# Gates and branch products of a hybrid trunk computed with tokens on the partitions, on one Trainium2 core

## The chip, the cores and the metric

The kernel runs on one core of one Trainium2 chip, as one program. The metric is the device time of one execution in microseconds (us). Three runs of the kernel before took 1461.19 to 1462.02 us, median 1461.55 us.

## The reference

A trunk of two layers over 256 tokens of width 1024, all in float32. Each layer is a half-weighted SwiGLU block, a mixer of three branches, and a second SwiGLU block. The mixer, cut to what matters:

```python
h = rms_norm(x, mix_norm[l])
rg_x, rg_g, sb_q, sb_k, sb_v, c_q, c_kv, k_r, gate_logits = split(h @ w_in[l])
y_a = rg_lru(conv(rg_x), ...) * gelu(rg_g)              # 1024 wide, a linear recurrence over tokens
y_b = stick_breaking_attention(sb_q, sb_k, sb_v)        # 8 heads of 128
y_c = mla_branch(c_q, c_kv, k_r, ...)                   # 8 heads, latent q and kv
g_a, g_b, g_c = split(sigmoid(gate_logits), 3)          # 1024 wide each
merged = g_a * (y_a @ w_branch_a) + g_b * (y_b @ w_branch_b) + g_c * (y_c @ w_branch_c)
x = x + merged @ w_out[l]
```

## The kernel before

Every float32 product is made of three products of split operands: a value is cast to a shorter one (`hi`) and the rest is kept (`lo`), and hi·hi, hi·lo and lo·hi are added. Weights come by DMA as one stream of tiles `raw`, four blocks of 128x512 at a time. For each pair of blocks (a piece) ScalarE casts `hi` and VectorE subtracts `lo` (`split_to`, `next_sub`), two pieces ahead of use. A block is called a sub.

TensorE's work is a list of groups. A feature group (`feature_group`) makes 256 output features with the features on the partitions: for each 128 of the contraction two matmuls of 512 columns (the weight's hi against the activations' hi and lo side by side) and two of 256 columns (the weight's lo against the activations' hi), so 32 matmuls for a contraction of 1024. Its two halves of the result are added at evacuation: a ScalarE copy, a VectorE add. A token group (`token_group`) makes 512 features with the tokens on the partitions: for each 128 of the contraction and each half of the tokens three matmuls of 512 columns (`mm3`), so 48 for a contraction of 1024, and the sum is complete in PSUM. Groups use two accumulators `acc` in turn; a group with a contraction of 256, and the last group of a stage, use two of four small banks `side`.

In the mixer, `MIX_ORDER` is a written-out order of the groups: `v`, `k`, `q`, `rgx`, `rgg`, `cq`, `ckv` from h; `uq`, `uqr`, `ukv`, `uv` from the latents; gates `ga`, `gb`, `gc`; branch products `bra`, `brb`, `brc`; `out`. The last digit is the number of the group. The three branches' own chains (`rg_chain`, `stick_pair`, `mla_pair`) run beside the groups as side tasks: their small matmuls, transposes, activations and vector work are issued between the groups' matmuls. What is issued when is decided while the program is built, by a clock of estimated costs (`Clock`, `Op`): after each step of a group `Tasks.tick` lets a side task issue an operation if its inputs are estimated to be ready, and at most a small amount of TensorE side work. Two calls issue side work without that test: `Tasks.wait`, when a group needs two `side` banks and fewer are free (`small_banks`), and `Tasks.drain`, when a group needs an operand that a task has not yet issued. On the chip each engine runs its instructions in the issued order and waits at each for its operands.

In `mix`, `gate(b, n)` evacuates a gate group, scales it by the norm's factor spread over partitions (`rb`) and takes tanh; `branch(i, b, n)` evacuates a branch product, forms (tanh + 1) times it and adds it to `merged[n]`; at the last branch of a group (i == 2) it casts and subtracts the sum into `mT[n]`, the operand pair of `out`. `update_x` adds an `out` group to x. Nearly all instructions carry the line of one helper, L201.

Of the kernel before, what the change touches and what calls it, by code (L numbers as in the profile page):

```python
# [6 lines left out]
F32 = mybir.dt.float32  # L7
# [7 lines left out]
NT = S // 128  # L15
# [13 lines left out]


MIX_ORDER = tuple((x.rstrip("0123"), int(x[-1])) for x in """
v0 k0 rgx0 rgx1 k1 q0 q1 cq0 q2 q3 k2 rgx2 v1 k3 rgx3 rgg0 rgg1 rgg2 rgg3
gb0 uq0 gb1 uq1 gb2 uq2 gb3 uq3 uqr0 brb0 brb1 ckv0 brb2 brb3 ga0 ukv0 ga1 ukv1 uv0 ga2 ukv2
ga3 ukv3 bra0 bra1 uv1 gc0 bra2 gc1 gc2 gc3 brc0 brc1 brc2 brc3 bra3 out0 out1 out2 out3
""".split())
C_C, C_G = 5120, 5696

FEATURES = {
    "rgx": ("in", 0, KD), "rgg": ("in", 1024, KD), "q": ("in", 2048, KD), "k": ("in", 3072, KD), "cq": ("in", C_C, KD),
    "ga": ("in", C_G, KD), "gb": ("in", C_G + 1024, KD), "gc": ("in", C_G + 2048, KD),  # L40
    "uq": ("uq", 0, 2), "ukv": ("ukv", 0, 2), "bra": ("bra", 0, KD), "brb": ("brb", 0, KD), "brc": ("brc", 0, KD), "out": ("out", 0, KD),
    "dn1": ("dn1", 0, KF), "dn2": ("dn2", 0, KF),
}
TOKENS = {"last": ("dn2", 0, KF), "v": ("in", 4096, KD), "uqr": ("uq", 1024, 2), "uv": ("ukv", 1024, 2)}


def group_stream(what, n):

    if what == "ckv":
        for k in range(0, 9, 3):  # L50
            yield ("ckv0", "in", k, C_C + 256)
            yield ("ckv1", "in", k, C_C + 256)
    elif what in TOKENS:
        m, c, nk = TOKENS[what]
        for k in range(nk):
            yield ("one", m, k, c + 512 * n)
    elif what in FEATURES:
        m, c, nk = FEATURES[what]
        for k in range(0, nk, 2):
            yield ("two", m, k, c + 256 * n)  # L60
    else:
        for k in range(0, KD, 2):
            yield ("gu", what, k, 128 * n)
# [274 lines left out]
def trunk(tc, xT_in, pos_in, w_in, rgw_in, fin_in, const_in, out):  # L338
# [4 lines left out]
    with ctx:  # L343
# [110 lines left out]
        def two(ap):  # L454
            return ap.rearrange("p (j t) -> p j t", j=2)
# [55 lines left out]
        def feature_group(kts, evac, last=0):  # L511


            nk = len(kts)
            a = small_banks() if last or nk <= 2 else bank()
            held = []
            for i, (h, _, hl) in enumerate(kts):
                if i % 2 == 0:
                    wh, wl = next_sub()
                held.append((i, h, hl, wh, wl))  # L520
                if nk - last <= i < nk - 1:
                    continue
# [8 lines left out]
            return finish(evac, a, tasks.LAST if last else None)  # L531

        def plain_group(c, xg, evac, norm):

# [656 lines left out]
        def mix(nm, ntasks, nxt, l):  # L1191
# [49 lines left out]
            merged, sig, mT = {}, {}, {}  # L1241

            def gate(b, n):
                def sigmoid(f):

                    act.activation(out=f, in_=f, func=AF.Tanh, scale=0.5)
                    yield
                    sig[b, n] = f

                def run(a):  # L1250
                    f = yield from scaled(a, mx["nm"], "rb")
                    yield
                    tasks.spawn(sigmoid(f))
                return run

            def branch(i, b, n):

                def run(a):
                    f = yield from FT.take()
                    hl = (yield from RT.take()) if i == 2 else None  # L1260
                    while (b, n) not in sig or (i and n not in merged):
                        yield 1
                    s = sig.pop((b, n))
                    m = merged[n] if i else None
                    for c, ap in parts(a):
                        fc, sc = two(f)[:, c], two(s)[:, c]
                        act.copy(fc, ap[:, :, 256:512])
                        dve.tensor_tensor(fc, ap[:, :, 0:256], fc, op=ALU.add)
                        if type(a) is not list:
                            yield  # L1270
                            give_banks(a)
                        dve.scalar_tensor_tensor(out=fc, in0=sc, scalar=1.0, in1=fc, op0=ALU.add, op1=ALU.mult)
                        if i:
                            mc = two(m)[:, c]
                            dve.tensor_tensor(mc, mc, fc, op=ALU.add)
                        if i == 2:
                            act.copy(hl[:, c, 0], mc)
                            dve.tensor_tensor(hl[:, c, 1], mc, hl[:, c, 0].bitcast(F32), op=ALU.subtract)
                    yield
                    if type(a) is list:  # L1280
                        give_banks(a)
                    FT.give(s)
                    if i == 0:
                        merged[n] = f
                        return
                    FT.give(f)
                    if i == 2:
                        FT.give(m)
                        mT[n] = hl
                return run  # L1290

            branches = [x for x in MIX_ORDER if x[0] in ("bra", "brb", "brc")]
# [14 lines left out]
            for g in MIX_ORDER:  # L1307
                what, n = g
                if what == "cq":
                    lt.append(narrow_group(kts, 256, w_cq, latents(mx, 0)))  # L1310
                elif what == "ckv":
                    lt.append(narrow_group(kts, 320, w_ckv, latents(mx, 1)))
                elif what == "uq":
                    feature_group(Latent(0), head_T(mx, "qn", n, "rbq"))
                elif what == "uqr":
                    token_group(Latent(0), q_rope(mx))
                elif what == "ukv":
                    feature_group(Latent(1), head_T(mx, "kn", n, "rbkv"))
                elif what == "uv":
                    token_group(Latent(1), head_v(mx, "v_ml", n, mx["rkv"]))  # L1320
                elif what == "rgx":
                    feature_group(kts, rg_x(mx, n))
                elif what == "rgg":
                    feature_group(kts, rg_g(mx, n))
                elif what == "v":
                    token_group(kts, head_v(mx, "v_sb", n, mx["rcol"]))
                elif what in ("q", "k"):
                    feature_group(kts, head_T(mx, what, n, "rb", SB_SCALE if what == "q" else None))
                elif what in ys:
                    mtask[n] = feature_group(Pairs(mx[ys[what]], lambda p: work[what][p:p + 1] if what == "bra" else work[what], KD), branch(turn[g], what[2], n), last=4 if g == branches[-1] else 0)  # L1330
                elif what == "out":
                    out_tasks.append(feature_group(Pairs(mT, lambda p: [mtask[p]], KD), lambda a, n=n: update_x(n, a, 0.5, nxt), last=4 if n == 3 else 0))
                else:
                    feature_group(kts, gate(what[1], n))
                if what in ys and n == 3:
# [182 lines left out]
```

## Time and profile before

| what | value |
|---|---|
| median of three runs | 1461.55 us |
| profiled execution, its own time | 1463.23 us |
| its span (first to last instruction) | 1461.4 us |
| TensorE matmul busy | 1442.5 us, 8276 matmuls |
| VectorE busy | 1108.8 us, 1548 instructions |
| ScalarE busy | 888.8 us, 1365 instructions |
| granted TensorE clock | 0.998 of full |
| mixer of layer 1, of layer 2 (from the first `v` matmul to the end of `out3`) | 349.92 us, 350.09 us |

A matmul's end is modelled in this profile and matmuls overlap, so a matmul's cost is read from the distance between starts and not from its busy time. Idle time of an engine is given with what ended it. The two mixers run the same program; the rows below are of the first one where it isn't said otherwise.

### The profile page before, as it was taken

The numbers are of one execution on the slowest core, as the hardware profiler recorded it, in microseconds if no ns is written. First come the engines' busy times: TensorE is split into PE (matmuls) and PEld (weight loads), VectorE is DVE, ScalarE is ACT, GpSimd is POOL, SyncE is SP. The second block draws the span as 40 slices with busy tenths as digits, with TensorE's granted clock in tenths as the row PEclk, the third lists the DMA queues.
The fourth block names the chain that finished last, engine by engine and source line by source line (L and its number), as shares of the span: only waits on it lengthen the run. The fifth ranks groups of instructions, "written<-read, shape, count | busy, mean of one in ns | idle before, by whom it ended". The sixth has DMA issues, their size and how long they took to land.

```text
span 1461.4 us, 20833 instructions
## 1 busy us (share of the span) xinstructions
PE 1442.5 (99%) x8276; PEld 1261.0 (86%) x8276; DVE 1108.8 (76%) x1548; ACT 888.8 (61%) x1365; POOL 144.5 (10%) x118
## 2 busy tenths in 40 slices
PE   8999999999999999999999999999999999999998
PEld 7888889888888888888888888898888888888886
DVE  5887567689987788876677776676989877877853
ACT  4665446888665556555455554479885656566543
POOL 2000001123410000000000000111323000100001
PEclk9999999999999999999999999999999999999999
DMA  6555554444543455455545455544444434545452
GB/s 244 201 185 192 200 179 163 170 151 147 197 148 145 171 179 194 179 200 178 198 173 201 177 198 184 200 159 155 141 171 174 173 138 166 199 175 201 176 199 87
DMA packets 37506, 258.17 MB, mean 177 GB/s; under 512 B 4256, under 2 KB 4640, under 8 KB 6816
## 3 DMA queue, kind: packets, MB, share of 16 engines
q1 hardware_dynamic: 35856, 253.16, 48.0%
q0 software_dynamic: 832, 2.62, 0.6%
q8 instruction: 65, 1.06, 0.3%
q10 hardware_dynamic: 720, 1.05, 0.2%
q14 instruction: 33, 0.27, 0.1%
HBM read 255.77 MB, written 1.05 MB: 176 GB/s over the span
## 4 chain that ended last, share of the span: by engine, by line
PE 90%; DVE 7%; issue 1%; ACT 1%; DMA 0%; ACTq 0%; POOLq 0%; POOL 0%; DVEq 0%
PE acc L201 76%; PE side L201 14%; DVE f L201 3%; DVE lo L201 3%; DVE r L201 1%; DMA x<-xT 0%; ACT f L201 0%; ACT hi L201 0%; ACT r L201 0%; ACTq L396 0%; POOLq L1514 0%; POOL rms L201 0%; DVE rms L201 0%; DVEq L201 0%
## 5 line engine op out<-in xcount | busy, mean ns | idle before, releaser
L201 PE MATMUL acc<-r,hi 128*128 128x512 f32 x3116 | 1000.3, 402 | 0.0
L201 DVE TENSOR_TENSOR lo<-raw,hi 128x1024 fp32r<-128x1024 f32 (+1 forms) x478 | 591.4, 1239 | 231.4 <-ACT hi L201 230.2
L201 PEld LDWEIGHTS acc<-r,lo 128*128 128x128 f32 x3116 | 585.2, 188 | 137.7
L201 PE MATMUL acc<-r,lo 128*128 128x256 f32 x3116 | 613.4, 278 | 0.0
L201 ACT CAST hi<-raw 128x1024 fp32r<-128x1024 f32 (+1 forms) x478 | 496.9, 1045 | 128.8 <-PE acc L201 91.9
L201 PEld LDWEIGHTS acc<-r,hi 128*128 128x128 f32 x3116 | 481.5, 189 | 5.0
L201 POOL TENSOR_TENSOR f<-f,f 128x512 f32<-128x512 f32 (+1 forms) x51 | 90.9, 1787 | 1043.3 <-ACT f L201 959.9
L201 ACT COPY f<-acc 128x512 f32<-128x512 f32 x164 | 96.0, 585 | 121.4 <-PE acc L201 121.2
L201 ACT ACTIVATE f<-f 128x256 f32<-128x256 f32 (+3 forms) x190 | 94.9, 502 | 85.6 <-DVE f L201 84.4
L201 DVE TENSOR_TENSOR f<-acc,f 128x512 f32<-128x512 f32 x166 | 113.9, 686 | 41.6 <-ACT f L201 41.2
L201 DVE TENSOR_TENSOR f<-f,f 128x512 f32<-128x512 f32 (+1 forms) x177 | 125.0, 706 | 7.8 <-ACT f L201 1.6
L201 ACT CAST r<-f 128x256 fp32r<-128x256 f32 (+2 forms) x130 | 58.7, 456 | 63.4 <-DVE f L201 59.7
L201 PE MATMUL acc<-hi,r 128*128 128x512 f32 (+2 forms) x344 | 96.9, 358 | 0.0
L201 PE MATMUL side<-r,hi 128*128 128x512 f32 x260 | 84.5, 396 | 0.0
L201 PE MATMUL side<-f,f 128*128 128x256 f32 (+1 forms) x320 | 71.7, 328 | 0.0
L201 PEld LDWEIGHTS acc<-hi,r 128*128 128x128 f32 x344 | 61.6, 189 | 8.3
L201 DVE TENSOR_TENSOR r<-f,r 128x256 fp32r<-128x256 f32 (+2 forms) x130 | 64.7, 502 | 1.9 <-ACT r L201 1.9
L201 PE MATMUL acc<-lo,r 128*128 128x512 f32 (+2 forms) x172 | 61.0, 355 | 0.0
L201 PE MATMUL side<-r,lo 128*128 128x256 f32 x260 | 60.5, 279 | 0.0
L201 PEld LDWEIGHTS side<-r,hi 128*128 128x128 f32 x260 | 45.6, 188 | 7.5
L201 PEld LDWEIGHTS side<-r,lo 128*128 128x128 f32 x260 | 47.0, 188 | 4.0
L201 PEld LDWEIGHTS side<-f,f 128*128 128x128 f32 x320 | 46.0, 191 | 0.5
(95 smaller groups left out, 839.1 us busy)
## 6 DMA issues: line engine op xcount, KB each, us to landing
raw<-w SPq DMA_DIRECT2D x239, 1024.0 KB, 4.8
f<-rgw POOLq DMA_DIRECT2D x8, 256.0 KB, 3.6
raw<-w SPq DMA_DIRECT2D x4, 256.0 KB, 5.7
out<-f SPq DMA_DIRECT2D x4, 256.0 KB, 2.2
x<-xT ACTq DMA_DIRECT2D x3, 256.0 KB, 6.9
f<-fin POOLq DMA_DIRECT2D x2, 256.0 KB, 3.4
cst<-const SPq DMA_DIRECT2D x1, 336.0 KB, 8.3
x<-xT ACTq DMA_DIRECT2D x2, 128.0 KB, 3.8
```

Of the source, the lines that this page charges most:

```text
L201: return self.f(*self.args, **self.kw)
```

## The change

Gates and branch products become token groups, two of 512 features each instead of four of 256. `gate` evacuates each half of the tokens with one ScalarE copy scaled by a per-token column and takes tanh. `branch` forms (tanh + 1) times the product straight from PSUM, and adds. At the last branch the sum, which has tokens on the partitions, is transposed by TensorE (`transpose_pair`, four 128x128 transposes into a `side` bank for each 256 features), and then cast and subtracted. `out0` and `out1` become one step, `outs0` (`feature_pair`): the first half of the contraction for both, then the second half for both. The order of the groups is new.

```diff
 MIX_ORDER = ...
-... rgg0 rgg1 rgg2 rgg3 / gb0 uq0 gb1 uq1 gb2 uq2 gb3 uq3 uqr0 brb0 ...
+... rgg0 rgg1 uq0 rgg2 uq1 rgg3 uq2 / gb0 uq3 gb1 uqr0 brb0 ckv0 brb1 ...
+        def feature_pair(kts, evacs):
+            nk = len(kts)
+            a = [bank() for _ in range(2)]
+            it = iter(kts)
+            for f in range(2):
+                half = [next(it) for _ in range(nk // 2)]
+                for n in range(2):
+                    for i, (h, _, hl) in enumerate(half, f * nk // 2):
...
+                        for b, c in enumerate(cs_):
+                            pe.matmul(a[n][:, b], wh[:, c], hl, start=i == 0, stop=False, skip_group_check=True)
+                        for b, c in enumerate(cs_):
+                            pe.matmul(a[n][:, b, 0:256], wl[:, c], h, start=False, stop=i == nk - 1, skip_group_check=True)
+                        tasks.tick()
+            return [finish(e, x) for e, x in zip(evacs, a)]
             def gate(b, n):
...
                 def run(a):
-                    f = yield from scaled(a, mx["nm"], "rb")
-                    yield
-                    tasks.spawn(sigmoid(f))
+                    fs = []
+                    for t in range(NT):
+                        f = yield from FT.take()
+                        act.activation(out=f, in_=bank_of(a, t), func=AF.Copy, scale=mx["rcol"][t])
+                        fs.append(f)
+                    yield
+                    give_banks(a)
+                    tasks.spawn(sigmoid(fs))
             def branch(i, b, n):
...
-                    for c, ap in parts(a):
-                        fc, sc = two(f)[:, c], two(s)[:, c]
-                        act.copy(fc, ap[:, :, 256:512])
-                        dve.tensor_tensor(fc, ap[:, :, 0:256], fc, op=ALU.add)
...
-                        if i == 2:
-                            act.copy(hl[:, c, 0], mc)
-                            dve.tensor_tensor(hl[:, c, 1], mc, hl[:, c, 0].bitcast(F32), op=ALU.subtract)
+                    for t, f in enumerate(fs):
+                        dve.scalar_tensor_tensor(out=f, in0=f, scalar=1.0, in1=bank_of(a, t), op0=ALU.add, op1=ALU.mult)
+                        if i:
+                            dve.tensor_tensor(merged[n][t], merged[n][t], f, op=ALU.add)
...
+                    if i == 2:
+                        for q in range(2):
+                            x = yield from transpose_pair(merged[n], q * 256)
+                            hl = yield from RT.take()
+                            hilo(x, hl)
+                            yield
+                            side.give(x)
+                            mT[2 * n + q] = hl
```

The first place is TensorE's order after the group `rgg1` of the first layer. `acc` is a group's accumulator, `side1_87` and `side3_89` are small banks in which two heads of the stick-breaking branch are summed, `r10_100` is a head's split operand that VectorE makes, `f6_112` and `f35_141` are what ScalarE makes of the two banks by an exponential, and `f12`, `f13` are values. Before:

```order
L201 MATMUL acc1_85<-r2_92,hi_2780 128x512 x2
L201 MATMUL acc1_85<-r2_92,lo_2781 128x256 x2
L201 MATMUL acc0_84<-r15_105,hi_2813 128x512 x2
L201 MATMUL acc0_84<-r15_105,lo_2814 128x256 x2
L201 MATMUL acc0_84<-r15_105,hi_2813 128x512 x2
L201 MATMUL acc0_84<-r15_105,lo_2814 128x256 x2
L201 MATMUL acc0_84<-r0_90,hi_2813 128x512 x2
L201 MATMUL acc0_84<-r0_90,lo_2814 128x256 x2
L201 MATMUL acc0_84<-r0_90,hi_2813 128x512 x2
L201 MATMUL acc0_84<-r0_90,lo_2814 128x256 x2
```

Here the whole group `rgg2` (32 matmuls into `acc0`) follows, and the two heads' matmuls stand singly at its end and within `rgg3`. The same place after, where L208 is the same helper:

```order
L208 MATMUL acc1_85<-r2_92,hi_2780 128x512 x2
L208 MATMUL acc1_85<-r2_92,lo_2781 128x256 x2
L208 MATMUL side1_87<-r6_96,tri_r_75 128x384 x2
L208 MATMUL side1_87<-f22_128,cst_72 128x128
L208 MATMUL side3_89<-r10_100,tri_r_75 128x384 x2
L208 MATMUL side3_89<-f27_133,cst_72 128x128
L208 MATMUL side2_88<-f35_141,f12_118 128x256
L208 MATMUL side2_88<-f35_141,f13_119 128x128
L208 MATMUL side2_88<-f6_112,f12_118 128x256
L208 MATMUL side2_88<-f6_112,f13_119 128x128
L208 MATMUL side1_87<-r11_101,hi_2813 128x512
L208 MATMUL side3_89<-r11_101,hi_2813 128x512
```

The ten side operations of two heads now stand in one piece ahead of `uq0`, whose matmuls are the last two rows and take the two banks that the heads give up; nothing of a large group lies between.

The second place is TensorE's order where the merged sums go into `out`. Before, the operands of `out0` (`r15`, `r0`) were made one to four groups earlier, and the last branch group `bra3` ends right ahead of it:

```order
L201 MATMUL side3_89<-r4_94,lo_4794 128x256 x2
L201 MATMUL side3_89<-r10_100,lo_4794 128x256 x2
L201 MATMUL acc1_85<-r15_105,hi_4817 128x512 x2
L201 MATMUL acc1_85<-r15_105,lo_4818 128x256 x2
L201 MATMUL acc1_85<-r15_105,hi_4817 128x512 x2
L201 MATMUL acc1_85<-r15_105,lo_4818 128x256 x2
```

After, the stretch is inside `outs0`, 28 matmuls behind its start; `f23_129` and `f12_118` are the merged sums of the second 512 features for the two halves of the tokens, `r4_94` is the first split operand made of them, and `cst` holds the identity:

```order
L208 MATMUL acc1_85<-r14_104,lo_4398 128x256 x2
L208 MATMUL side1_87<-cst_72,f23_129 128x128
L208 MATMUL acc1_85<-r14_104,hi_4397 128x512 x2
L208 MATMUL acc1_85<-r14_104,lo_4398 128x256 x2
L208 MATMUL side1_87<-cst_72,f12_118 128x128
L208 MATMUL side1_87<-cst_72,f23_129 128x128
L208 MATMUL side1_87<-cst_72,f12_118 128x128
L208 MATMUL side0_86<-cst_72,f23_129 128x128
L208 MATMUL side0_86<-cst_72,f12_118 128x128
L208 MATMUL side0_86<-cst_72,f23_129 128x128
L208 MATMUL side0_86<-cst_72,f12_118 128x128
L208 MATMUL acc0_84<-r4_94,hi_4434 128x512 x2
```

The eight transposes of the second half of the sums stand in the middle of `outs0`, and the first matmul that uses their result follows them at once.

## Rows read from the trace of the kernel before

**Rows 1.** The page: busy time, share of the span and instructions of two engines.

```profile
PE   1442.5 (99%) x8276; PEld 1261.0 (86%) x8276; DVE 1108.8 (76%) x1548; ACT 888.8 (61%) x1365; POOL 144.5 (10%) x118
```

**Rows 2.** The chain that ended last: start us, us, engine, tile, line, count.

```profile
356.56 5.57 PE acc L201 x32
```

**Rows 3.** Timeline of TensorE, a token group alone: start us, us, operation, shapes, count.

```profile
1399.71 0.62 PE L201 MATMUL acc<-hi,r 128*128 128x512 f32 x2
...
1422.83 0.62 PE L201 MATMUL acc<-hi,r 128*128 128x512 f32 x2
```

**Rows 4.** Timeline of TensorE, the token group `v0` in the mixer.

```profile
207.86 0.63 PE L201 MATMUL acc<-hi,r 128*128 128x512 f32 x2
...
209.25 0.63 PE L201 MATMUL acc<-hi,r 128*128 128x512 f32 x2
```

**Rows 5.** Timeline of TensorE, four transposes of x between feature steps.

```profile
1294.59 0.71 PE L201 MATMUL acc<-r,hi 128*128 128x512 f32 x2
...
1295.38 0.60 PE L201 MATMUL side<-cst,x 128*128 128x128 f32 x4
1295.73 0.71 PE L201 MATMUL acc<-r,hi 128*128 128x512 f32 x2
```

**Rows 6.** Timeline of TensorE in `rgg3`; in brackets idle time and its releaser.

```profile
335.23 0.36 PE L201 MATMUL side<-r,r 128*128 128x256 f32 x1
336.47 0.39 PE L201 MATMUL side<-r,r 128*128 128x256 f32 x1 [0.88 <-DVE r L201]
...
338.57 0.28 PE L201 MATMUL side<-r,r 128*128 128x256 f32 x1
340.31 0.62 PE L201 MATMUL side<-r,r 128*128 128x256 f32 x3 [1.46 <-DVE r L201]
```

**Rows 7.** Timeline of TensorE in `brb3`.

```profile
402.29 0.40 PE L201 MATMUL acc<-r,lo 128*128 128x256 f32 x2
403.73 0.70 PE L201 MATMUL side<-f,cst 128*128 128x256 f32 x2 [1.04 <-DVE f L201]
```

**Rows 8.** Timeline of all engines, from the end of `rgg1` on.

```profile
323.09 0.62 PE L201 MATMUL acc<-r,hi 128*128 128x512 f32 x2
...
326.39 1.21 DVE L201 TENSOR_TENSOR lo<-raw,hi 128x1024 fp32r<-128x1024 f32 x1
...
327.52 0.68 DVE L201 TENSOR_TENSOR f<-acc,f 128x512 f32<-128x512 f32 x1
...
328.24 0.69 DVE L201 TENSOR_TENSOR f<-f,f 128x512 f32<-128x512 f32 x1
```

**Rows 9.** Timeline of all engines, the same heads' matmuls in `rgg3`.

```profile
330.38 0.97 DVE L201 TENSOR_TENSOR r<-f,r 128x384 fp32r<-128x384 f32 x1
...
331.34 0.51 PE L201 MATMUL side<-r,tri_r 128*128 128x384 f32 x2
331.69 0.38 PE L201 MATMUL side<-f,cst 128*128 128x128 f32 x2
...
332.17 0.49 ACT L201 ACTIVATE f<-side 128x384 f32<-128x384 f32 x1 [0.25 <-PE side L201]
```

**Rows 10.** VectorE's groups of one shape: count, busy us, mean ns, idle before.

```profile
L201 DVE TENSOR_TENSOR lo<-raw,hi 128x1024 fp32r<-128x1024 f32 x474 | 588.3, 1242 | 229.7 <-ACT hi L201 228.4
...
L201 DVE TENSOR_TENSOR f<-acc,f 128x512 f32<-128x512 f32 x166 | 113.9, 686 | 41.6 <-ACT f L201 41.2
...
L201 DVE TENSOR_TENSOR r<-side,r 128x512 fp32r<-128x512 f32 x16 | 10.9, 683 | 5.1 <-ACT r L201 5.1
...
L201 DVE TENSOR_TENSOR r<-f,r 128x384 fp32r<-128x384 f32 x16 | 9.5, 602 | 0.0
```

**Rows 11.** ScalarE's groups of one shape.

```profile
L201 ACT CAST r<-side 128x512 fp32r<-128x512 f32 x16 | 9.4, 586 | 17.3 <-PE side L201 17.2
```

**Rows 12.** Timeline of all engines, two transposes and the copy behind them.

```profile
407.76 0.38 PE L201 MATMUL side<-cst,f 128*128 128x128 f32 x2
...
408.23 0.75 ACT L201 COPY f<-side 64x256 f32<-64x256 f32 x2 [1.96 <-PE side L201]
```

More of the change, by code (lines that the diff above doesn't have):

```diff
@@ L31 @@
 MIX_ORDER = tuple((x.rstrip("0123"), int(x[-1])) for x in """
-v0 k0 rgx0 rgx1 k1 q0 q1 cq0 q2 q3 k2 rgx2 v1 k3 rgx3 rgg0 rgg1 rgg2 rgg3
-gb0 uq0 gb1 uq1 gb2 uq2 gb3 uq3 uqr0 brb0 brb1 ckv0 brb2 brb3 ga0 ukv0 ga1 ukv1 uv0 ga2 ukv2
-ga3 ukv3 bra0 bra1 uv1 gc0 bra2 gc1 gc2 gc3 brc0 brc1 brc2 brc3 bra3 out0 out1 out2 out3
+v0 k0 rgx0 rgx1 k1 q0 q1 cq0 q2 q3 k2 rgx2 v1 k3 rgx3 rgg0 rgg1 uq0 rgg2 uq1 rgg3 uq2
+gb0 uq3 gb1 uqr0 brb0 ckv0 brb1 ukv0 ga0 ukv1 uv0 ga1 ukv2 bra0 ukv3 uv1 gc0 gc1 bra1 brc0 brc1
+outs0 out2 out3
 """.split())
@@ L39 @@
     "rgx": ("in", 0, KD), "rgg": ("in", 1024, KD), "q": ("in", 2048, KD), "k": ("in", 3072, KD), "cq": ("in", C_C, KD),
-    "ga": ("in", C_G, KD), "gb": ("in", C_G + 1024, KD), "gc": ("in", C_G + 2048, KD),
-    "uq": ("uq", 0, 2), "ukv": ("ukv", 0, 2), "bra": ("bra", 0, KD), "brb": ("brb", 0, KD), "brc": ("brc", 0, KD), "out": ("out", 0, KD),
+    "uq": ("uq", 0, 2), "ukv": ("ukv", 0, 2), "out": ("out", 0, KD),
     "dn1": ("dn1", 0, KF), "dn2": ("dn2", 0, KF),
 }
-TOKENS = {"last": ("dn2", 0, KF), "v": ("in", 4096, KD), "uqr": ("uq", 1024, 2), "uv": ("ukv", 1024, 2)}
+TOKENS = {"last": ("dn2", 0, KF), "v": ("in", 4096, KD), "uqr": ("uq", 1024, 2), "uv": ("ukv", 1024, 2),
+    "ga": ("in", C_G, KD), "gb": ("in", C_G + 1024, KD), "gc": ("in", C_G + 2048, KD),
+    "bra": ("bra", 0, KD), "brb": ("brb", 0, KD), "brc": ("brc", 0, KD),
+}
 def group_stream(what, n):
@@ L52, in group_stream @@
             yield ("ckv1", "in", k, C_C + 256)
+    elif what == "outs":
+        for h in range(2):
+            for n in range(2):
+                for k in range(KD // 2 * h, KD // 2 * (h + 1), 2):
+                    yield ("two", "out", k, 256 * n)
     elif what in TOKENS:
@@ L531, in feature_group @@
             return finish(evac, a, tasks.LAST if last else None)
+        def feature_pair(kts, evacs):
[4 more added lines that the diff above has]
+                half = [next(it) for _ in range(nk // 2)]
+                for n in range(2):
+                    for i, (h, _, hl) in enumerate(half, f * nk // 2):
+                        if i % 2 == 0:
+                            wh, wl = next_sub()
+                        cs_ = [slice((i % 2) * 256 + b * 128, (i % 2) * 256 + (b + 1) * 128) for b in range(2)]
+                        for b, c in enumerate(cs_):
[4 more added lines that the diff above has]
+            return [finish(e, x) for e, x in zip(evacs, a)]
         def plain_group(c, xg, evac, norm):
@@ L1243, in gate, with sigmoid @@
             def gate(b, n):
-                def sigmoid(f):
-                    act.activation(out=f, in_=f, func=AF.Tanh, scale=0.5)
+                def sigmoid(fs):
+                    for f in fs:
+                        act.activation(out=f, in_=f, func=AF.Tanh, scale=0.5)
                     yield
-                    sig[b, n] = f
+                    sig[b, n] = fs
                 def run(a):
-                    f = yield from scaled(a, mx["nm"], "rb")
+                    fs = []
[3 more added lines that the diff above has]
+                        fs.append(f)
                     yield
-                    tasks.spawn(sigmoid(f))
+                    give_banks(a)
+                    tasks.spawn(sigmoid(fs))
                 return run
@@ L1279, in run @@
-                    yield
[L1280 to L1289, printed above, removed]
+                    fs = sig.pop((b, n))
+                    for t, f in enumerate(fs):
+                        dve.scalar_tensor_tensor(out=f, in0=f, scalar=1.0, in1=bank_of(a, t), op0=ALU.add, op1=ALU.mult)
+                        if i:
+                            dve.tensor_tensor(merged[n][t], merged[n][t], f, op=ALU.add)
@@ new lines, in run @@
+                    yield
+                    give_banks(a)
+                    if i == 0:
+                        merged[n] = fs
+                        return
+                    FT.give(*fs)
+                    if i == 2:
[3 more added lines that the diff above has]
+                            hilo(x, hl)
+                            yield
+                            side.give(x)
+                            mT[2 * n + q] = hl
+                        FT.give(*merged[n])
@@ L1329, in mix @@
                 elif what in ys:
-                    mtask[n] = feature_group(Pairs(mx[ys[what]], lambda p: work[what][p:p + 1] if what == "bra" else work[what], KD), branch(turn[g], what[2], n), last=4 if g == branches[-1] else 0)
+                    mtask[n] = token_group(Pairs(mx[ys[what]], lambda p: work[what][p:p + 1] if what == "bra" else work[what], KD), branch(turn[g], what[2], n), last=4 if g == branches[-1] else 0)
+                elif what == "outs":
+                    out_tasks += feature_pair(Pairs(mT, lambda p: [mtask[p // 2]], KD), [lambda a, n=n: update_x(n, a, 0.5, nxt) for n in range(2)])
                 elif what == "out":
-                    out_tasks.append(feature_group(Pairs(mT, lambda p: [mtask[p]], KD), lambda a, n=n: update_x(n, a, 0.5, nxt), last=4 if n == 3 else 0))
+                    out_tasks.append(feature_group(Pairs(mT, lambda p: [mtask[p // 2]], KD), lambda a, n=n: update_x(n, a, 0.5, nxt), last=4 if n == 3 else 0))
                 else:
-                    feature_group(kts, gate(what[1], n))
-                if what in ys and n == 3:
+                    token_group(kts, gate(what[1], n))
+                if what in ys and n == 1:
                     RT.give(*mx[ys[what]].values())
```

10 lines of the change are left out of this document (removed).

## The prediction

> **What bounds the kernel now.** I read the page's busy shares first: TensorE's matmuls are busy for 99% of the span, VectorE 76%, ScalarE 61% [rows 1]. Since a matmul's end is modelled there, I then read starts in the timeline, to see what TensorE pays for a group when nothing is late: 32 matmuls of a feature group take 5.57 us [rows 2], and three matmuls of a token group 0.68 us (34 of them from 1399.71 to 1422.83) [rows 3]. Third come TensorE's idle times with their releasers. In a mixer there are only three that count. Two matmuls of the recurrence wait for VectorE's `r` in `rgg3`: the next start comes 1.24 and 1.74 us later where 0.12 is the step, so 1.12 and 1.62 us are lost [rows 6]; and in `brb3` the spread of the norm waits for VectorE's `f`, 1.44 us where 0.23 is the step, 1.21 us lost [rows 7]. That is 3.95 us per mixer. All else in a mixer is TensorE going from one matmul to the next. So time moves only by the number and kind of matmuls, and by waits of TensorE that go or come. VectorE and ScalarE count where TensorE waits for them.
>
> **TensorE's stream.** Per layer 24 feature groups go: 24 x 5.57 = 133.7 us [rows 2]. Twelve token groups come, each 8 steps x 2 halves x 0.68 = 10.88 us: 130.6 us [rows 3]. That is -3.1 us. Sixteen transposes of 128x128 come. Four of them between two feature steps stretch the way from 1294.59 to 1295.73, 1.14 us, where four matmuls take 0.70 (a feature group's eighth) [rows 2, 5]: 0.11 us each, 1.76 us per layer. Stream: -1.35 us per layer. Bounds: in the mixer's own `v0` six matmuls take 1.39 us instead of 1.36 [rows 4]; at that pace a token group takes 11.12 us and -3.1 becomes -0.3. I take the long stretch, since `v0`'s distance is read next to a side operation.
>
> The Trainium skill, "TensorE: Matmul & The Clock Gate", section Part 4: PE-mode transpose, puts a transpose of this size at about 275 ns in a kernel's context. The profile has the same length for one but starts them 0.11 us apart, so that length overlaps; by the page's figure the 32 transposes of both layers would be an estimated 8.8 us instead of 3.5, and the sum below 5.3 us higher.
>
> **What leaves VectorE and ScalarE.** A gate loses an add and a scaling on VectorE, a branch product an add and a ScalarE copy. Per layer that is some 25 us of VectorE (24 adds of 0.69 us [rows 10] and 12 scalings of about the same), from behind TensorE's 99%. I cost it at nothing, except that it may end waits. DMA: the weights come in another order but in the same tiles and number, through SP's queue as before, and no transfer is on TensorE's waits.
>
> **The old waits.** The recurrence's matmuls of `rgg3` now stand in `gb0`, behind `uq0`, `uq1`, `uq2` and two gelu groups, by when VectorE has caught up (below). The norm's spread stands at the end of `brb1`, three token steps (4.1 us) behind VectorE's last instruction for it, and VectorE has had less to do from `gb0` on. I take both away: -3.95 us per layer. At worst the recurrence keeps its 2.74.
>
> **The new wait at `uq0`.** `uq0` takes two small banks, and in the new order fewer than two are free, so ten side operations of two heads are issued in one piece ahead of it. Up to the end of `rgg1` both kernels issue the same, so the rows give the start: TensorE is done with `rgg1` at 323.09, and VectorE, some 3 us behind, is free for its next instruction at 326.39 [rows 8]. Now that is not the weight's `lo` but the evacuation of `rgg1` (two steps, 0.72 apart [rows 8]: 0.72 + 0.70) and then the head's `r10` (0.60 [rows 10]): 328.4. Behind it, as before, 0.83 us pass from the head's first matmul to the start of the exponential, which takes 0.49 [rows 9]: 329.7. Then two float32 matmuls with the values, an estimated 0.65 us from the 128-column one's two passes of 0.11 (331.69 to 331.83 and one more) [rows 9]: `uq0` starts at 330.4, 7.3 us after 323.09. The ten operations are 2.4 us of work that was there before (four of 0.17, two of 0.22, two pairs of 0.65). 4.9 us is wait. Before, the 32 matmuls of `rgg2` and 12 of `rgg3` covered it; that cover is gone. Everything behind on TensorE's queue waits: `uq0`, then `rgg2`. ScalarE's and VectorE's queues hold the head's evacuation `r4` until 331, then VectorE has some 13 us of work (five `lo` of 1.24 and the steps of four groups [rows 10]) for the 14 us that TensorE takes to the recurrence's matmuls (two large and two small groups), which is why I take the old wait as gone. Bounds: 0.8 us if VectorE were not behind (the round trip over ScalarE less the matmuls that fill it), 5.3 if `r10` takes the 0.97 that it took beside GpSimd's work [rows 9]. I take 4.9, since VectorE's rows to 326.39 are the same instructions.
>
> **The new wait in `outs0`.** Let T be the last matmul of the last branch group. Four transposes of the first half's sums follow (0.44), ScalarE starts 0.36 after the last one's start [rows 12], its cast takes 0.59 [rows 11]; VectorE's subtraction (0.68) ends at T + 2.0. Behind it on VectorE's queue stand a `lo` (1.24) and the four steps of the last evacuation (0.72, 0.61, 0.72, 0.69) [rows 8, 10], to T + 5.8, and a second `lo`, to T + 6.9. On TensorE the second operand of `outs0` is wanted at T + 1.83: 0.2 us lost. The first half of `outs0` with the eight transposes of the second sums ends at T + 7.1. Their first cast starts at T + 6.9 and ends at T + 7.5, the subtraction at T + 8.2: 1.15 us lost. Sum 1.35 us. Before, `out0` began with sums made groups earlier. Bounds: 0, if the evacuation gets ahead of the `lo`s; 2.5, if one more `lo` falls ahead of the subtraction.
>
> **The new wait at `uv1`.** It too asks for two banks; only ScalarE and VectorE steps are issued for it. Its first bank is freed by a subtraction that stands behind the four steps of `bra0`'s evacuation: 0.2 + 2.74 + 0.68 = 3.6 us after `bra0`'s last matmul [rows 8, 10], while TensorE has about 3.0 us of work in between. 0.6 us; bounds 0 and 1.3 (two more evacuation steps).
>
> **Sum.** Per layer -1.35 - 3.95 + 4.9 + 1.35 + 0.6 = +1.55 us, for two layers +3.1. Against the profiled execution's own 1463.23 us (span 1461.4 and 1.8 around it) that is 1466.3; that execution lies 1.7 above the median of the three runs, so against the median, 1461.55 + 3.1 = 1464.6 us.
>
> **Rivals.** (1) Not slower: the pieces at `uq0` are less late. It decides at VectorE's `r10`: each us that VectorE reaches it earlier than 328.4 takes a us off. If it gets there by 327.4 and the other two new waits hide, the layer is -1.35 - 3.95 + 3.9 = -1.4, 1458.8 us. For it: 25 us of VectorE work go. Against it: none of that work stands ahead of `uq0`; the first gate comes after. (2) VectorE stays behind: the recurrence's wait (2.74 per layer) moves to `gb0` instead of ending, and GpSimd's work slows VectorE there as in [rows 9]: +5.5, 1470.1 us. For it: VectorE idles for 3 us at `uq0`, waiting for the head. Against: a 32-matmul group gives it 5.57 us for two `lo` and two evacuation steps, 3.9 us [rows 10]. (3) The change doesn't do what it says: token groups are no cheaper than feature groups here, as at the pace of `v0`. Then the stream is +1.45 per layer, the sum +8.7, 1470.2 us. For it: `v0` is the only one in a mixer that was read. The Trainium skill, same page, section Back-to-back issue gap, has a formula by columns, N / 2.4 + 2.5 ns, by which both kinds of group would cost about the same; the distances of [rows 2, 3] don't follow it, the feature group being dearer by 2%.
>
> **How the numbers follow.** No change is within 0.2%, 1458.6 to 1464.5 us, about what a measurement of this kernel can tell. Forecast 0.64: its own range is 1461.5 to 1467.5, the middle just over the bound, so I split it 0.34 slower, 0.30 same. Rival (1) 0.16: 0.11 faster, 0.05 same. Rival (2) 0.12 and rival (3) 0.08: slower. Faster 0.11, same 0.35, slower 0.54. Range 1460 to 1469.5: it leaves out the far ends of rival (1), and of (2) and (3) about half.
>
> **What would show it.** Right: TensorE idle by 4 to 5 us ahead of `uq0`'s first side matmul, with VectorE's `r` and ScalarE's `f` as releasers, in both layers; idle of about 1 us in the middle of `outs0` behind the eight transposes, released by `r`; none at the recurrence's matmuls and the norm's spread; token groups of gates at 10.9 us. Wrong: an idle time over 1 us that is none of these, an idle time under 3 us at `uq0`, or transposes more than 0.2 us apart.

## The result, and the profile after

The changed kernel is slower: 1469.55 us (median of 4 runs, 1467.72 to 1471.06) against 1461.78 us of the kernel before, run beside it (4 runs, 1461.19 to 1463.03). The ratio is 1.0051, 95% interval [1.0034, 1.0069], so +7.8 us where +3.1 was forecast, at the very end of the range (1469.5). The four runs lie in two pairs, 1467.72 and 1468.04 us, and 1471.05 and 1471.06 us at a slightly lower mean granted clock (0.997 against 0.995 to 0.996), and the profiled one is of the lower pair.

The profiled execution took 1468.04 us, with a span of 1466.3 us, 4.9 more than before. The two mixers account for more than that: from the first matmul of `v0` to the end of `out3` they take 353.6 us each, where they took 349.9 and 350.1, +3.6 and +3.5, 7.1 us in sum. The other 2.2 us lie ahead of the first mixer, most of them at the start, where the profiled execution of the kernel before ran 3.4 us at half clock. The first row is that of before, the second that of after (stretch, its length, busy time of PE, PEld, DVE, ACT, POOL, then the granted clock, 0.50 being 1.2 GHz, the DMA's share and its GB/s):

```profile
10.80:14.20 3.40, 3.22 (x8) 2.49 (x8) 3.40 (x11) 3.14 (x7) 1.11 (x2) 0.50 1.04 434
```

```profile
10.80:14.20 3.40, 3.40 (x16) 3.01 (x17) 3.40 (x8) 2.72 (x7) 1.38 (x2) 1.00 1.04 431
```

The page of after, against [rows 1]: VectorE lost 44 us of work, TensorE's share stayed at 99%, and no average tells where 7 us went.

```profile
PE 1445.8 (99%) x7924; PEld 1246.4 (85%) x7924; DVE 1064.3 (73%) x1468; ACT 876.0 (60%) x1337; POOL 135.5 (9%) x118
```

TensorE's waits of after, summed by releaser (total us, times, longest). Those of [rows 6, 7] are gone; these came, each twice (once per layer) or four times:

```profile
PE side L208 <- ACT r L208: 4.6, 2, 2.3
PE side L208 <- DVE r L208: 4.4, 4, 1.7
PE acc L208 <- DVE r L208: 1.9, 2, 1.0
```

Where they stand is in TensorE's timeline. First the place of `uq0` (start, length, operation; in brackets idle time and releaser), which answers to [rows 8, 9]:

```profile
320.92 0.52 PE L208 MATMUL side<-r,tri_r 128*128 128x384 f32 x2
321.27 0.38 PE L208 MATMUL side<-f,cst 128*128 128x128 f32 x2
323.96 0.44 PE L208 MATMUL side<-r,tri_r 128*128 128x384 f32 x1 [2.30 <-ACT r L208]
326.10 0.44 PE L208 MATMUL side<-r,tri_r 128*128 128x384 f32 x1 [1.70 <-DVE r L208]
326.38 0.38 PE L208 MATMUL side<-f,cst 128*128 128x128 f32 x2
326.60 2.56 PE L208 MATMUL side<-f,f 128*128 128x256 f32 x8
328.82 1.20 PE L208 MATMUL side<-r,hi 128*128 128x512 f32 x2
...
330.95 0.40 PE L208 MATMUL acc<-r,hi 128*128 128x512 f32 x1
```

Two things are to be seen. TensorE stands for the head's `r` twice, 2.5 and 2.0 us in starts. The first time it waits for the half that ScalarE casts, and that cast had itself waited 1.65 us for VectorE; the second time for the half that VectorE makes, which stands behind VectorE's evacuation of `rgg1`:

```profile
323.40 0.51 ACT L208 CAST r<-f 128x384 fp32r<-128x384 f32 x1 [1.65 <-DVE f L208]
...
324.18 0.68 DVE L208 TENSOR_TENSOR f<-acc,f 128x512 f32<-128x512 f32 x1
324.89 0.69 DVE L208 TENSOR_TENSOR f<-f,f 128x512 f32<-128x512 f32 x1
325.50 0.55 DVE L208 TENSOR_TENSOR r<-f,r 128x384 fp32r<-128x384 f32 x1
```

And behind the second wait the matmuls are slow: two of `uq0` last 1.20 us where two of the same shape last 0.62 to 0.73 elsewhere. The stretches by granted clock say why. A fall of the same length stands at `uq0` of the second layer; before, no mixer had one.

```profile
318.00:326.80 8.80, 4.79 (x30) 4.05 (x29) 8.01 (x11) 3.69 (x8) 5.50 (x4) 1.00 0.35 119
326.80:330.20 3.40, 3.40 (x12) 2.89 (x11) 0.37 (x1) 1.49 (x3) 0.00 (x0) 0.50 0.00 0
330.20:340.00 9.80, 9.80 (x58) 8.54 (x57) 7.79 (x10) 8.66 (x13) 1.93 (x2) 1.00 0.24 73
...
1050.43:1053.84 3.41, 3.41 (x13) 2.95 (x12) 0.00 (x0) 0.79 (x2) 0.00 (x0) 0.50 0.00 0
```

The Trainium skill, "TensorE: Matmul & The Clock Gate", section Why this matters for your kernels, asks to leave TensorE no long idle gaps between bursts of matmuls, since its clock falls to half behind one. The trace agrees in that the fall stands behind idle times, here two of 2.30 and 1.70 us with one matmul between them; an experiment below has more idle time in sum, 5.1 us of 14, without such a fall.

The other two new waits are in the middle of `outs0`, behind the second set of transposes, and at `uv1`:

```profile
530.90 0.93 PE L208 MATMUL side<-cst,f 128*128 128x128 f32 x7
532.79 0.73 PE L208 MATMUL acc<-r,hi 128*128 128x512 f32 x2 [0.96 <-DVE r L208]
```

```profile
453.17 0.60 PE L208 MATMUL side<-f,f 128*128 128x256 f32 x2
454.26 0.50 PE L208 MATMUL side<-hi,r 128*128 128x512 f32 x1 [0.50 <-DVE r L208]
```

Last, the stream: in the chain of waits a gate group without side work (`gb1`) stands as one piece of 48 matmuls, which answers to [rows 2, 3]:

```profile
358.87 10.89 PE acc L208 x48
```

### The profile page after: what moved, and what is told of

Its sections match the earlier page's. It is cut to its first block, busy times and chain, and to the rows that moved or that the text cites. A ratio compares the mean times of both kernels' runs of the same rounds, so it can differ in the third digit from the quotient of the medians.

```text
span 1466.3 us, 20030 instructions
## 1 busy us (share of the span) xinstructions
PE 1445.8 (99%) x7924; PEld 1246.4 (85%) x7924; DVE 1064.3 (73%) x1468; ACT 876.0 (60%) x1337; POOL 135.5 (9%) x118
## 4 chain that ended last, share of the span: by engine, by line
PE 96%; DVE 3%; DMA 0%; issue 0%; ACT 0%; ACTq 0%; POOLq 0%; POOL 0%
PE acc L208 80%; PE side L208 16%; DVE f L208 2%; DVE r L208 1%; DMA x<-xT 0%; DVE lo L208 0%; ACT r L208 0%; ACTq L403 0%; ACT f L208 0%; POOLq L1539 0%; POOL rms L208 0%; DVE rms L208 0%
## 5 line engine op out<-in xcount | busy, mean ns | idle before, releaser
L208 DVE TENSOR_TENSOR lo<-raw,hi 128x1024 fp32r<-128x1024 f32 (+1 forms) x478 | 595.5, 1249 | 266.5 <-ACT hi L208 265.0
L208 PE MATMUL acc<-r,hi 128*128 128x512 f32 x2380 | 757.0, 399 | 1.9 <-DVE r L208 1.9
L208 ACT CAST hi<-raw 128x1024 fp32r<-128x1024 f32 (+1 forms) x478 | 495.7, 1045 | 133.0 <-PE acc L208 97.5
L208 PEld LDWEIGHTS acc<-r,lo 128*128 128x128 f32 x2380 | 447.0, 188 | 105.3
L208 PE MATMUL acc<-r,lo 128*128 128x256 f32 x2380 | 468.2, 278 | 0.0
L208 PEld LDWEIGHTS acc<-r,hi 128*128 128x128 f32 x2380 | 364.9, 189 | 4.7 <-DVE r L208 2.8
L208 PE MATMUL acc<-hi,r 128*128 128x512 f32 (+2 forms) x1048 | 340.5, 391 | 0.0
L208 PEld LDWEIGHTS acc<-hi,r 128*128 128x128 f32 x1048 | 193.9, 188 | 34.9
L208 PE MATMUL acc<-lo,r 128*128 128x512 f32 (+2 forms) x524 | 198.5, 379 | 0.0
L208 POOL TENSOR_TENSOR f<-f,f 128x512 f32<-128x512 f32 (+1 forms) x51 | 85.6, 1687 | 1052.0 <-ACT f L208 703.7
L208 ACT ACTIVATE f<-f 128x256 f32<-128x256 f32 (+3 forms) x190 | 94.3, 501 | 73.4 <-DVE f L208 72.2
L208 ACT COPY f<-acc 128x512 f32<-128x512 f32 x118 | 69.0, 585 | 97.3 <-PE acc L208 97.3
L208 PEld LDWEIGHTS acc<-lo,r 128*128 128x128 f32 x524 | 98.8, 189 | 15.5
L208 DVE TENSOR_TENSOR f<-f,f 128x512 f32<-128x512 f32 (+1 forms) x151 | 105.4, 698 | 6.9 <-ACT f L208 1.6
L208 DVE TENSOR_TENSOR f<-acc,f 128x512 f32<-128x512 f32 x120 | 82.3, 686 | 34.5 <-ACT f L208 34.2
L208 ACT CAST r<-f 128x256 fp32r<-128x256 f32 (+2 forms) x120 | 53.3, 449 | 51.0 <-DVE f L208 47.5
L208 PE MATMUL side<-r,hi 128*128 128x512 f32 x228 | 76.6, 406 | 0.0
L208 PE MATMUL side<-f,f 128*128 128x256 f32 (+1 forms) x320 | 73.1, 336 | 0.0
L208 PE MATMUL side<-hi,r 128*128 128x512 f32 x200 | 64.9, 394 | 1.0 <-DVE r L208 1.0
L208 DVE TENSOR_TENSOR r<-f,r 128x256 fp32r<-128x256 f32 (+2 forms) x120 | 55.8, 470 | 0.0
L208 PEld LDWEIGHTS side<-f,f 128*128 128x128 f32 x320 | 51.1, 196 | 4.8
L208 PE MATMUL side<-r,lo 128*128 128x256 f32 x228 | 53.6, 279 | 0.0
```

What stands on the lines that cost most here:

```text
L208: return self.f(*self.args, **self.kw)
```

## The experiments

Theory A: the change pays at `uq0`, by the wait and by the half clock behind it. Theory B: the token groups or the pair of outputs pay, and `uq0` only shows it. All runs were timed against the kernel before (1461.2 to 1461.5 us).

**`uq` groups late.** The changed kernel with one part of the order put back:

```
-... rgx3 rgg0 rgg1 uq0 rgg2 uq1 rgg3 uq2
-gb0 uq3 gb1 uqr0 ...
+... rgx3 rgg0 rgg1 rgg2 rgg3
+gb0 uq0 uq1 gb1 uq2 uq3 uqr0 ...
```

> The changed kernel with uq0 to uq3 back among the gate groups (rgg0 to rgg3 in a row, then gb0 uq0 uq1 gb1 uq2 uq3 uqr0); all else stays. Theory A (the early place of uq0 is what the change pays for: 6.2 us per layer, 4.4 of waiting and the rest a stretch at half clock): no wait of over 1 us and no half-clock stretch at uq0, so 2 x 6.2 = 12.4 us go, and the recurrence's old wait in rgg3 (2.74 per layer) may come back since the order there is that of before: 1457 if it stays away, 1462.6 if it comes back whole. Theory B (the place of uq0 only uncovers waiting that the token groups or the pair of outputs cause anyway): the waits turn up elsewhere, 1467 to 1470.

Measured: 1474.0 us, ratio to before 1.0096 [1.0082, 1.0109], slower than the changed kernel. Theory A fails in this form. The wait and the half clock at `uq0` did go and the old waits of [rows 6] came back, 0.87 and 1.48 us, as expected; but `uqr0`, the group behind `uq3`, waits 1.45 us for VectorE in both layers, and in `brb1` of the first layer the transposes of branch c's rotated queries (`q_rope`) wait 2.83 us, with a half-clock stretch (`brb1` takes 17.5 us where 11.7 in the changed kernel):

```profile
397.88 0.90 PE L208 MATMUL side<-cst,f 128*128 128x128 f32 x3 [2.83 <-DVE f L208]
```

```profile
397.30:400.70 3.40, 2.82 (x8) 2.35 (x9) 2.65 (x5) 1.56 (x4) 0.00 (x0) 0.50 0.59 193
```

So with token groups the late places are dearer than the early ones. What makes the rotated queries late was not tested; in the trace VectorE had itself stood 2.79 us for ScalarE ahead of them, and ScalarE 3.31 us for GpSimd.

**`uq` groups early, alone.** The kernel before, feature groups kept, with this order:

```
-... rgg0 rgg1 rgg2 rgg3
-gb0 uq0 gb1 uq1 gb2 uq2 gb3 uq3 uqr0 ...
+... rgg0 rgg1 uq0 rgg2 uq1 rgg3 uq2
+gb0 uq3 gb1 gb2 gb3 uqr0 ...
```

> The kernel before with uq0, uq1 and uq2 alone moved ahead, to the places that they have in the changed kernel; gates, branch products and outputs as before. Theory A: the wait at uq0 and the half-clock stretch come as in the changed kernel, 2 x 6.2 = 12.4 us; the recurrence's waits in rgg3 go (2 x 2.74 = 5.5 back), the norm's spread in brb3 may keep its 1.2: 1461.8 + 12.4 - 5.5 = 1468.7, with 1466.3 if the spread's wait goes too. Theory B: within 1 us of the kernel before, 1461 to 1463.

Measured: 1473.34 us, 1.0087 [1.0073, 1.0101]. The spread's wait is gone as well, so A's figure is 1466.3, and the run is 7.0 us over it. In the first layer `uq0`'s place takes 10.06 us, in the changed kernel 10.03, with the same two waits and the same fall:

```profile
324.69 0.44 PE L201 MATMUL side<-r,tri_r 128*128 128x384 f32 x1 [2.30 <-ACT r L201]
326.83 0.69 PE L201 MATMUL side<-r,tri_r 128*128 128x384 f32 x1 [1.71 <-DVE r L201]
```

Thus that wait needs neither token groups, transposes nor the pair. The miss is a new wait of 2.0 us for `r` at `brc0`, in both layers, and in the second layer a half-clock stretch there and a longer one at `uq0` (6.83 us, and 10.81 us for the place). Both experiments point the same way: a place in the order has no price of its own; moving one group changes what covers the others.

**`out0` and `out1` one after the other.**

```
-outs0 out2 out3
+out0 out1 out2 out3
```

> The changed kernel with out0 and out1 one after the other in place of outs0. Theory A: the pair only covers the second half's sums; out0 alone reaches its second half after 16 of its 32 matmuls, 2.8 us instead of 5.6 after its start, so its wait grows from 1.0 to 2 to 3.8 us per layer: 2 to 5.6 us over the changed kernel, 1471.6 to 1475. Theory B (the pair costs, since its matmuls or its two evacuations at once are what is slow): same or up to 2 us faster, 1467.5 to 1469.6.

Measured: 1478.15 us, 1.0118 [1.0104, 1.0132], 8.6 us over the changed kernel. The direction is A's, the size beyond it. In place of one wait of 0.96, `out0` has three for `r`, and its transposes wait for `f`:

```profile
528.16 0.70 PE L208 MATMUL acc<-r,hi 128*128 128x512 f32 x2 [2.18 <-DVE r L208]
530.71 0.55 PE L208 MATMUL side<-cst,f 128*128 128x128 f32 x3 [0.81 <-DVE f L208]
532.66 0.74 PE L208 MATMUL acc<-r,hi 128*128 128x512 f32 x2 [1.40 <-DVE r L208]
535.47 0.72 PE L208 MATMUL acc<-r,hi 128*128 128x512 f32 x2 [0.70 <-DVE r L208]
```

In the second layer a half-clock stretch follows these waits; in the first layer none does, though TensorE is busy for only 8.93 us of 14:

```profile
526.00:540.00 14.00, 8.93 (x50) 7.36 (x51) 11.04 (x14) 5.41 (x9) 0.00 (x0) 1.00 0.27 98
```

Another 1.6 us stand at `uq0`, although the instructions there are those of the changed kernel: in both layers the half clock lasts 6.83 us there in place of 3.41, and the place takes 10.51 and 11.17 us in place of 10.03 and 10.06. In the first layer the clock falls ahead of the first waiting matmul (323.00):

```profile
322.80:329.60 6.80, 5.14 (x15) 4.19 (x16) 2.38 (x5) 1.77 (x5) 0.21 (x1) 0.50 0.26 110
```

So the length of a fall is not fixed by the order of the work.

**Filler in the waits at `uq0`.** The changed kernel, and ahead of the two waiting matmuls:

```
...
+def filler(i):
+    for _ in range({2: 14, 3: 10}.get(i, 0)):
+        nc.tensor.matmul(acc.free[0][:, 0, 0:384], ident_b, cbf.rearrange("p a b -> p (a b)"), start=True, stop=True)
...
```

> The changed kernel with filler matmuls that compute nothing, 384 columns of bf16 each, put on TensorE's queue in the two waits ahead of uq0 (14 in the first, 10 in the second; some 2.2 and 1.6 us of work in waits of 2.5 and 2.0), into the accumulator that rgg2 overwrites. The waits stay, since ScalarE and VectorE are as late as before. Theory A: the clock falls because TensorE stands idle there, so with the filler it stays at full speed from 326.8 to 330.2 and in the second layer, and 2 x 1.7 = 3.4 us go: 1466.1. Rival C: the fall of the clock has nothing to do with these waits: it stays, 1469.5. Rival D: the waits are longer than the profile says since TensorE's start is what sets ScalarE's exponential; then no more than 1 us goes.

Measured: 1464.85 us, 1.0025 [1.0014, 1.0035], 4.7 below the changed kernel. No mixer has a half-clock stretch any more, and the waiting matmuls start as long after the place's first matmul as before (3.03 and 5.19 us, in the changed kernel 3.04 and 5.18):

```profile
321.73 0.52 PE L208 MATMUL side<-r,tri_r 128*128 128x384 f32 x2
...
322.30 2.44 PE L502 MATMUL acc<-cbf 128*128 128x384 bf16 x14
324.76 0.44 PE L208 MATMUL side<-r,tri_r 128*128 128x384 f32 x1
325.05 1.80 PE L502 MATMUL acc<-cbf 128*128 128x384 bf16 x10
326.92 0.44 PE L208 MATMUL side<-r,tri_r 128*128 128x384 f32 x1
...
330.37 0.40 PE L208 MATMUL acc<-r,hi 128*128 128x512 f32 x1
```

From the second waiting matmul to `rgg2` it is 3.45 us in place of 4.85. So this fall costs 1.40 us per layer, 2.8 in sum (by the mixers 1.3 per layer, 352.2 us in place of 353.6), and it follows from TensorE standing idle: the same waits filled with useless work do not bring it. (The timed 4.7 is more than the 2.8 of the traces; the intervals of the two ratios, some 1.5 and 2.5 us to either side, allow it.) Rivals C and D fall.

**VectorE's work ahead of `uq0` taken away.** The changed kernel without six convolution taps; the planner still counts them, so that no other instruction moves:

```
...
-... op0=ALU.mult, op1=ALU.add)
+... op0=ALU.mult, op1=ALU.add, skip=p == 3)
```

> The changed kernel without VectorE's six convolution taps of the last quarter of the recurrence's channels (that part of the computation is left out); every other instruction stands where it stood. Four of the six stand on VectorE's queue between rgg0 and the head's r ahead of uq0, and take 0.4 + 0.4 + 1.4 + 0.9 = 3.1 us of its time there. Theory A (VectorE's lag decides the wait at uq0): TensorE's two waits of 2.5 and 2.0 us shrink by 2.2 to 3.1 us in sum, and if the clock then stays at full speed by up to 1.5 us more: 2 x (2.2 to 4.6) = 4.4 to 9.2 us, 1460 to 1465. Rival (the round trip of the head over ScalarE decides, VectorE only stands last in the record): within 1 us of the changed kernel, 1468.5 to 1470.

Measured: 1462.58 us, 1.0010 [1.0001, 1.0019], 7.0 below the changed kernel, within A's bounds. The waits fall from 2.30 and 1.70 to 0.80 and 1.36, by 1.84 in sum, less than the 2.2 to 3.1 that A gave, and the clock stays at 1.00:

```profile
322.51 0.44 PE L208 MATMUL side<-r,tri_r 128*128 128x384 f32 x1 [0.80 <-ACT r L208]
324.31 0.44 PE L208 MATMUL side<-r,tri_r 128*128 128x384 f32 x1 [1.36 <-DVE r L208]
```

The place takes 6.80 us, 3.2 less: 1.84 of wait and 1.40 of half clock. VectorE's `r` is done 3.29 us after the place's first matmul, in the changed kernel 5.13 us, so the waits shrank by just what VectorE gained: VectorE's lag behind TensorE decides them. It gained less than the 3.1 us of the taps, since two of its other instructions took longer than in the changed kernel, a weight's `lo` 2.31 us for 1.21 and the evacuation's second step 1.23 for 0.69, both beside GpSimd's work.

**`uq0` on accumulator banks.** Nothing is forced ahead of it then:

```
...
-a = small_banks() if last or nk <= 2 else bank()
+a = small_banks() if small and (last or nk <= 2) else bank()
...
```

> The changed kernel with uq0 alone on a pair of accumulator banks, as a large group has, in place of two small banks; so nothing has to be issued ahead of it and the heads' steps stay among the steps of rgg2. Theory A, in its narrow form (the price is that the ten steps are forced ahead): uq0 starts at once, rgg2 then waits for rgg1's accumulator, which VectorE reads until 324.9, 2.4 us behind uq0's last matmul; 6.2 becomes 2.4, and 1469.5 - 7.6 = 1462. In its wide form (VectorE's lag behind TensorE is the price, whoever asks first): TensorE waits 4 to 6 us for the accumulator or at uq1 in place of uq0, and the clock falls behind that as well: 1467 to 1471.

Measured: 1479.47 us, 1.0122 [1.0108, 1.0136]. Not the forcing, but the lag is the price: with nothing forced, `rgg2` waits 3.58 us for the accumulator that VectorE has not read, and the clock is at half for 6.8 us in the first layer and 3.4 in the second. The transposes of branch c's rotated queries come late as well (a wait of 2.9 us for `f` and another half-clock stretch in each layer), so it is more than the wide form's 1471.

```profile
326.02 1.22 PE L208 MATMUL acc<-r,hi 128*128 128x512 f32 x2 [3.58 <-DVE f L208]
```

```profile
325.16:332.00 6.84, 5.98 (x20) 5.41 (x21) 6.77 (x9) 3.19 (x5) 2.52 (x2) 0.50 0.04 14
```

**Another order for the changed kernel.** I replayed each kernel's instruction order on in-order engines with the durations of the trace and looked for an order with few waits; nothing but the order changes:

```
+v0 k0 rgx0 rgx1 k1 q0 q1 cq0 k2 rgx2 q2 q3 v1 rgx3 rgg0 rgg1 k3 rgg2 uq1 gb0 gb1 uq0
+rgg3 uq2 brb0 uq3 uqr0 ckv0 ga0 ukv0 brb1 uv0 ukv1 ukv2 bra0 uv1 ga1 ukv3 gc0 gc1 brc0 brc1 bra1
 outs0 out2 out3
```

> The changed kernel with the groups in another order; token groups, transposes and the pair stay. k2, rgx2 go ahead of q2, q3; k3 stands between rgg1 and rgg2; rgg2, uq1, gb0 and gb1 come before uq0, rgg3 after it; brb1 and ga1 stand later, bra1 behind brc1. uq0 then has rgg2 and two gate groups of cover, and fewer heads' steps are pending when it asks for its banks. Theory A (what the change pays is waits that its order uncovers, while its stream is shorter by about 0.9 us per layer): the waits at uq0, in outs0 and at brb1 are mostly gone and no half-clock stretch stands in a mixer; at best the mixer is 353.6 - 6.2 - 1.6 - 0.7 = 345.1 us, 8.5 per layer less, 1452.5; about half of that, 1461, where one new wait of 3 to 4 us per layer comes. Theory B (the waits belong to the token groups and only move): 1467 or more, as in the order with uq0 late (1474).

Measured: 1456.48 us, 0.9966 [0.9952, 0.9979]: 13 us under the changed kernel, 4.7 under the kernel before, the fastest of all. The mixer takes 348.0 us. No mixer has a half-clock stretch; of TensorE's waits one of 1.0 us in `outs0` and one of 0.4 us for ScalarE's `f` are left in each layer; those for DMA and for `tiny` stand at the program's start:

```profile
PE acc L208 <- DVE r L208: 1.9, 2, 1.0
PE acc L208 <- DMA raw<-w: 1.2, 1, 1.2
PE side L1377 <- DVE tiny L1394: 1.0, 1, 1.0
PE side L208 <- ACT f L208: 0.9, 2, 0.4
```

**The same search for the kernel before.** Feature groups, its groups in the order that came out best:

```
+v0 k0 rgx0 rgx1 k1 q0 q1 cq0 q2 q3 rgx2 k2 v1 k3 gb0 rgg2 gb2 rgx3 rgg1 gb1 uq2 rgg0 rgg3 uq1 uqr0 gb3 uq0 brb0 ...
```

> The kernel before with its groups in another order, chosen by the same measure as the order that brought the changed kernel to 1456.5 (few waits in a replay of the instruction order with measured durations); gates, branch products and outputs stay feature groups without transposes. Theory A (the order is what brings the gain of that kernel, and the token groups bring their shorter stream, 0.9 us per layer, and VectorE's relief): faster than the kernel before, but behind that kernel, 1457 to 1460. Rival (the token groups are what let the order work, since VectorE has some 25 us less to do per layer): no faster than before, 1460 to 1465. Rival (the token groups bring nothing): as fast or faster than 1456.5.

Measured: 1461.19 us, 0.9996 [0.9987, 1.0005]: no change. The second expectation holds, as far as one order can show it. In the program it has five side waits for `f` and four for `r`, none over 1.2 us, and its mixer takes 349.9 us as before:

```profile
PE side L200 <- DVE r L200: 3.1, 4, 1.2
PE side L200 <- DVE f L200: 3.0, 5, 0.9
```

**The pair undone in the fastest kernel.** As in the third experiment, `outs0` becomes `out0 out1`.

> The order that brought the changed kernel to 1456.5, with out0 and out1 one after the other in place of outs0. In the changed kernel's own order that cost 8.6 us. Theory A (the pair gives the second half of the sums 2.8 us more of cover; the rest of the 8.6 was a half-clock stretch behind the longer wait): 2 to 4 us per layer again, 1460.5 to 1464.5. Rival (in an order in which VectorE is on time the sums are ready anyway): within 1 us of 1456.5.

Measured: 1462.51 us, 1.0008 [0.9999, 1.0017], 6.0 over the fastest kernel, within A's bounds; the mixers take 351.2 and 350.4 in place of 348.0, in the first with a half-clock stretch of 3.41 us behind the waits. The pair is worth 2.4 us in the layer without a fall and 3.2 in the one with it.

## Why the prediction was right and wrong

Right was that the kernel gets slower, and at which places it waits: no idle time over 1 us stands elsewhere in the mixers. The step that failed is the new wait at `uq0`, and in it the price: the wait was counted, the half clock behind it was not. Per layer, from the timelines:

- **The wait at `uq0`**: predicted 4.9. The place takes 10.03 us; less the 1.39 of `uq0` itself, the ten operations' 2.4 of the prediction and the half clock's 1.40, 4.84 us are left, 2.5 and 2.0 of them in the two waits for `r`. VectorE's part came as worked out, the evacuation of `rgg1` and then the head's `r`, done 5.1 us after the place's start where the prediction had 5.3. ScalarE's exponential `f`, forecast as a releaser, is none: TensorE finds work in its round trip, slowed by the half clock, and with the filler it stands there for 0.15 us. Instead TensorE waits earlier, for ScalarE's cast of `r`.
- **Not in the sum**: the half clock, 1.40 us (the filler run), 2.8 for both layers. The granted clock of the kernel before is whole in its mixers, and I carried that over to an order with a wait of a kind that the mixers had not had. None of my rivals and none of my bounds for `uq0` (0.8 to 5.3) had it.
- **`outs0`**: predicted 1.35, measured 1.6 (13.63 us less 64 matmuls at 0.174, 11.14, and eight transposes at 0.11). The steps that the prediction lists from T + 2.0 add up to T + 6.0, where it has T + 5.8. **`uv1`**: predicted 0.6, measured 0.66 (from 453.17 to 454.26, less two float32 passes of some 0.22).
- **The old waits**: both gone, -3.95, as predicted.
- **The stream**: predicted -1.35. A gate group takes 10.89 us and a transpose 0.11, as read before; the Trainium skill's 275 ns for a transpose (same page, section Part 4: PE-mode transpose) again is not their distance. What is left of the mixer's +3.55 us when the terms above are taken off, 3.55 + 3.95 - 4.84 - 1.40 - 1.6 - 0.66, is -1.0. It was not measured by itself, and small stretches next to side work are in it. In the fastest kernel the same count leaves +0.3 (347.97 less 1.24 in `outs0` and 0.44 for `f`, against 349.92 less 3.95), so a shorter stream is not shown, and what that kernel gains over the kernel before is waits.

So 4.0 us were missing in both layers: 2.8 of half clock, 0.7 of stream, 0.5 in `outs0`, 0.1 at `uv1`, and 0.1 too much at the wait for `r`. With them the 3.1 become the 7.1 of the traces, by construction, since the stream is what the others leave; the 7.8 timed agree within their interval.

Of the rivals, (1) didn't come: VectorE was as late as said. (2) "VectorE stays behind" gave nearly the measured time, 1470.1, by luck: its mechanism did not occur, since the recurrence's waits are gone. (3) didn't come as stated, since a gate group takes 10.89 us; that the whole stream got shorter is not shown either.

The cover that hid VectorE's relief is shown only in part. The changed kernel's 22 us per layer less on VectorE (25 were forecast) bring nothing to be seen in its own order, but in another order the same instructions beat the kernel before by 4.7 us, and feature groups in an order found by the same means do not. That the token groups are why is likely, but rests on one order for each.

## What to carry to other kernels

A wait that a new order opens on TensorE costs its length and, where the clock falls behind it, that too; look at the granted clock of the stretch after the wait, and give such a fall a term or a rival even if the kernel before shows none. Relief of an engine that is not the bound brought no gain here until the order was tuned again for it: first see at which waits that engine stands last, then move groups there as cover. And undoing one part of a change does not give that part's price, if the other parts moved the cover that it needs.

## What the runs showed of the hardware

- The clock fell to 0.50 for 3.41 us, beginning 0.70 us after TensorE's second wait at `uq0` ended (326.10 to 326.80), with 2.5 and 2.0 us of standing before it; with waits of 0.80 and 1.36 us, or with filler in the longer ones, it did not. With the same instructions up to there, in the third experiment, it fell at 322.80, in the first wait, and for 6.83 us. In the wait for the accumulator it fell at 325.16, ahead of the next matmul at 326.02, and for 6.8 us.
- The same waits are not always followed by a fall: in `out0` of the third experiment, 5.1 us of idle time in 14 left the clock at 1.00 in the first layer, while in the second layer the same three waits for `r` had a fall of 3.41 us with them.
- A VectorE tap of the convolution took 0.4 us of its queue's time, and 0.9 to 1.4 where a TENSOR_TENSOR on GpSimd ran beside it. Of the four ahead of `uq0`, those at 313.06 and 317.10, with GpSimd idle, took 0.4 each; those at 318.68 and 323.29, with GpSimd busy from 318.30 to 319.91 and from 322.46 to 323.97, took 1.4 and 0.9. This adds an estimated 1.5 us to VectorE's lag, from these four numbers.
